# Two cached pages per item: the second page's table read and load on the GpSimd queue

## The chip, the cores and the metric

One core of a Trainium2 chip runs the whole program. The time is that of the device, in microseconds (us), of one execution. The kernel before took 1503.48, 1509.17 and 1512.21 us in three runs, median 1509.17. Engines: PE (TensorE, matrix products), DVE (VectorE), ACT (ScalarE), POOL (GpSimd), SP (SyncE, which here only issues DMAs). TensorE's clock has two levels, 1.2 and 2.4 GHz; the profile gives the granted clock as a share of the upper one.

## The reference

One step of a two-layer decoder for a prompt of 256 tokens and 8 samples with 8 new tokens each, which share all weights; 320 token columns in all. The first layer projects the input once and feeds two branches:

- an attention of 8 heads. The prompt attends to itself, with a relative bias. Each sample attends to its own 8 tokens and to 2048 cached tokens, of which the three best blocks of 256 keys per query are chosen by the product of the query with the block's mean key. The cache is paged: 128 tokens to a page, 16 pages to a sample, found by a table of page numbers;
- an mLSTM with a matrix memory, of 4 heads.

The core of the sample branch in the reference's terms:

```python
k_mean = jnp.mean(kb.astype(f32), axis=2)            # blocks of 256 keys
gate = jnp.einsum('bthd,bnhd->bhtn', q.astype(f32), k_mean)
sel_val, sel_idx = lax.top_k(gate, n_sel)            # three blocks
p = softmax(concat([s_own, s_sel]))                  # own tokens and chosen blocks
o = p_own @ v_own + p_sel @ v_sel
```

The second layer is a gated short convolution. Both end in a layer norm over a scaled residual. The outputs are the activations, the new keys and values, and the new mLSTM and convolution states.

## The kernel before

Everything that TensorE multiplies comes through one stream of items of 512 KB, each loaded into one of 11 buffers called `raw`. An item is half of a weight tile (`lin_load`, one DMA), two cached pages of keys or of values (`k_load`, `v_load`, two DMAs of 256 KB), or a state of the mLSTM (`state_item`, two DMAs of 256 KB). Weight halves are split into a high part `sh` (ACT) and a low part `sl` (DVE) before TensorE uses them (`split`); pages are used as they are.

The pages are read in four units of 4 samples and 4 heads. A unit has 32 key items (8 blocks of 256 keys for 4 samples) and 32 value items, so there are 128 items of each, and 512 page loads in all. The program puts 4 page items in a bunch and then two or three weight halves, in the order K0 K1 V0 K2 V1 K3 V2 V3 (K0: the keys of unit 0). This stage lies at about 42 to 800 us of the span; after it only weights and states are loaded.

The order on each engine is written out once, when the program is built. The loop `ahead` starts the load of an item as soon as its buffer has been freed in that order, and it calls the item's `load`. What an engine's queue holds is therefore in the order in which the functions were called, and each engine works through its queue strictly in that order. All page loads, weight loads and state loads stand in SP's queue. A page load has its page number read from the table `pt` first: `page` (L454) makes a register load on the queue's engine, register arithmetic and a check of the range (three instructions), then L461 or L469 issues the DMA.

POOL's queue holds the small transfers, in this order by the program: `rel` (L330) and `dt15` (L333), the rows of the relative bias; for each head the stores of keys `k_o` (L354, L355) and of values `v_o` (L365), and the bias rows `bt` of the prompt's head (L406, in `prompt_head`); then `hn` and `n0` (L657, L658), the mLSTM's segment mask and state, with some memsets; `kd` and `vd` (L803, L829), mLSTM moves; stores of states. In `prompt_head` the load of `bt` is the first instruction. DVE then adds it to TensorE's scores in `pS`, and TensorE transposes `pS` (out `mB` or `mC`, from `cst,pS`). The function is started after the value tile of its head has been stored.

Of the kernel before, what the change touches and what calls it, by code (L numbers as in the profile page):

```python
# [36 lines left out]
NPG = 16  # L37
NPOOL = 160
# [112 lines left out]
def trunk_kernel(ctx, tc, x_in, kc, vc, pages, cst_in, seg_in, hot_in, small_in, c0_in, n0_in, w_in,  # L151
                 y_out, k_out, v_out, cp_out, cs_out, n_out, m_out, conv_out):
    nc = tc.nc
# [35 lines left out]
    pt = pc.tile([1, NB * NPG], I32, name="pt")  # L189
# [260 lines left out]
    units = [Unit(n) for n in range(4)]  # L450
    pv_groups = [0]

    def page(b, j):
        return nc.sync.value_load(pt[0:1, b * NPG + j:b * NPG + j + 1], min_val=0, max_val=NPOOL - 1)  # L454

    def k_load(u, blk, b4):
        def f(raw):
            r = raw.rearrange("p (g f) -> p g f", g=2)
            for j in range(2):
                n = page(4 * u.quad + b4, 2 * blk + j)  # L460
                nc.sync.dma_start(r[:, j, :], kc[bass.ds(n, 1), u.half].rearrange("o p f -> (o p) f"))  # L461
        return f

    def v_load(u, b4, pp):
        def f(raw):
            r = raw.rearrange("p (g f) -> p g f", g=2)
            for j in range(2):
                n = page(4 * u.quad + b4, 2 * pp + j)
                nc.sync.dma_start(r[:, j, :], vc[bass.ds(n, 1), :, 512 * u.half:512 * u.half + 512]  # L469
                                  .rearrange("o p f -> (o p) f"))  # L470
        return f

# [1035 lines left out]
    for ft in range(KT):  # L1508
# [5 lines left out]
        o = M[:, ft, :]  # L1514
        c = 16 + ft
        g, b = small[:, S_LG + c:S_LG + c + 1], small[:, S_LB + c:S_LB + c + 1]
# [128 lines left out]
```

## Time and profile before

| | us |
|---|---|
| runs (median of 3) | 1503.48 to 1512.21 (1509.17) |
| the profiled execution | 1510.37 |
| its span | 1508.6 |
| PE busy | 1462.5 (97%) |
| DVE busy | 776.0 (51%) |
| ACT busy | 598.1 (40%) |
| POOL busy | 128.1 (8%) |

The span is the time between the first and the last instruction of the profiled execution. Busy means that an instruction was running; the times in which an engine stood still, and what ended each of them, are in the views of the waits. The DMA share is the mean busy share of the core's 16 DMA engines. An issue on SP or POOL is only the instruction that starts a DMA; its data land later.

### The profile page before, as it was taken

What the parts mean: (1) busy time and instruction counts of PE and PEld (TensorE: products, weight loads), DVE (VectorE), ACT (ScalarE), POOL (GpSimd) and SP (SyncE); (2) the same over time, 40 slices, a digit from 0 to 9 for tenths busy, and PEclk for the clock granted to TensorE, in tenths of its full rate; (3) what the DMA queues carried; (4) which work ended last, traced back from release to release, by engine and by line L of the source; (5) the groups of instructions that cost most, each with busy time, mean ns of one, the idle gap of its engine ahead of it and who ended that gap; (6) DMA issues with size and microseconds to landing.
All of it is one profiled execution on the core that took longest, in us unless ns stands there. A gap on an engine that the chain in (4) does not pass through costs nothing.

```text
span 1508.6 us, 31980 instructions
## 1 busy us (share of the span) xinstructions
PE 1462.5 (97%) x11983; PEld 1372.1 (91%) x11983; DVE 776.0 (51%) x1296; ACT 598.1 (40%) x1124; POOL 128.1 (8%) x244
## 2 busy tenths in 40 slices
PE   9899999999989999799989999999999999999998
PEld 9688889888879788699889999999999999999998
DVE  5234334433333423243256865777766666666665
ACT  5233534433233433243254444444443333333444
POOL 0200000010001010000001006223110000000000
PEclk9999999999989999999999999999999999999999
DMA  9799989989899999899884546777656444444412
GB/s 325 252 323 309 304 270 312 300 273 308 297 304 304 303 320 301 273 310 310 274 312 146 199 170 185 242 227 220 227 200 196 141 140 162 145 140 157 155 43 70
DMA packets 150957, 356.43 MB, mean 236 GB/s; under 512 B 24453, under 2 KB 30854, under 8 KB 150802
## 3 DMA queue, kind: packets, MB, share of 16 engines
q1 hardware_dynamic: 130946, 325.65, 64.3%
q0 software_dynamic: 19856, 28.74, 6.7%
q8 instruction: 94, 1.54, 0.4%
q14 instruction: 61, 0.50, 0.1%
HBM read 337.31 MB, written 16.98 MB: 235 GB/s over the span
## 4 chain that ended last, share of the span: by engine, by line
PE 74%; issue 12%; DMA 7%; ACT 2%; DVE 2%; SPq 1%; POOL 1%; ACTq 0%; POOLq 0%; DVEq 0%
PE lin L164 64%; PE kv L164 6%; DMA raw<-w_all 3%; PE mB L164 2%; DMA bt<-rel 1%; ACT sh L86 1%; PE mC L164 1%; DMA M<-x_in 1%; DVE sl L86 1%; POOL Xl L1263 1%; SPq L454 1%; PE mB L169 1%; DMA vd<-vms 1%; SPq L469 1%; DVE M L86 0%
## 5 line engine op out<-in xcount | busy, mean ns | idle before, releaser
L86 DVE TENSOR_TENSOR sl<-raw,sh 128x1024 fp32r<-128x1024 f32 (+1 forms) x341 | 412.0, 1215 | 521.0 <-ACT sh L86 518.2
L86 ACT ACTIVATE sh<-raw 128x1024 fp32r<-128x1024 f32 (+1 forms) x341 | 354.0, 1046 | 460.9 <-DMA raw<-w_all 264.0
L164 PE MATMUL lin<-Xh,sh 128*128 128x320 f32 x1648 | 526.0, 319 | 10.2 <-ACT sh L86 8.5
L164 PE MATMUL lin<-Xh,sl 128*128 128x320 f32 x1648 | 512.8, 311 | 4.7 <-DVE sl L86 4.7
L164 PE MATMUL lin<-Xl,sh 128*128 128x320 f32 x1648 | 511.8, 311 | 0.5 <-DVE Xl L86 0.5
L164 PEld LDWEIGHTS lin<-Xh,sh 128*128 128x128 f32 x1648 | 311.9, 189 | 32.5 <-issue 13.8
L164 PE MATMUL lin<-X2h,sh 128*128 128x322 f32 x1024 | 318.5, 311 | 0.0
L164 PEld LDWEIGHTS lin<-Xh,sl 128*128 128x128 f32 x1648 | 311.7, 189 | 7.0 <-DVE sl L86 6.9
L164 PE MATMUL lin<-X2l,sh 128*128 128x322 f32 x1024 | 317.8, 310 | 0.0
L164 PE MATMUL lin<-X2h,sl 128*128 128x322 f32 x1024 | 317.6, 310 | 0.0
L164 PEld LDWEIGHTS lin<-Xl,sh 128*128 128x128 f32 x1648 | 312.0, 189 | 1.6 <-DVE Xl L86 1.0
L164 PEld LDWEIGHTS lin<-X2l,sh 128*128 128x128 f32 x1024 | 193.8, 189 | 0.1
L164 PEld LDWEIGHTS lin<-X2h,sh 128*128 128x128 f32 x1024 | 192.8, 188 | 0.1
L164 PEld LDWEIGHTS lin<-X2h,sl 128*128 128x128 f32 x1024 | 192.5, 188 | 0.0
L164 PE MATMUL kv<-raw,PT 128*32 128x128 f32 x2048 | 69.0, 276 | 4.5 <-DMA raw<-vc 4.5
L164 PE MATMUL kv<-raw,qp 128*32 128x256 f32 x1024 | 65.5, 390 | 7.3 <-issue 7.3
L164 PEld LDWEIGHTS kv<-raw,PT 128*32 128x32 f32 x2048 | 54.2, 110 | 15.3 <-DMA raw<-vc 8.2
L164 PEld LDWEIGHTS kv<-raw,qp 128*32 128x32 f32 x1024 | 29.6, 111 | 30.0 <-issue 15.0
L86 ACT ACTIVATE sg<-sg 128x320 f32<-128x320 f32 x71 | 33.3, 469 | 13.1 <-DVE sg L86 11.5
L86 ACT ACTIVATE lnq<-M 128x320 f32<-128x320 f32 x30 | 14.1, 472 | 59.0 <-DVE M L86 59.0
L86 DVE SCALAR_TENSOR_TENSOR z<-lnc,ze,lin 128x320 f32<-128x320 f32 x64 | 34.7, 543 | 2.2 <-ACT ze L86 2.2
L86 DVE TENSOR_TENSOR z<-z,lny 128x320 f32<-128x320 f32 x64 | 31.5, 492 | 2.2
(311 smaller groups left out, 1006.6 us busy)
## 6 DMA issues: line engine op xcount, KB each, us to landing
raw<-w_all SPq DMA_DIRECT2D x335, 512.0 KB, 4.9
raw<-kc SPq DMA_DIRECT2D x256, 256.0 KB, 4.4
raw<-vc SPq DMA_DIRECT2D x256, 256.0 KB, 4.5
raw<-c SPq DMA_DIRECT2D x32, 256.0 KB, 5.6
xr<-c POOLq DMA_DIRECT2D x32, 256.0 KB, 4.6
cs_o<-xr POOLq DMA_DIRECT2D x32, 256.0 KB, 4.2
xr<-x_in POOLq DMA_DIRECT2D x16, 160.0 KB, 3.3
y_o<-M SPq DMA_DIRECT2D x16, 160.0 KB, 1.8
```

What stands on the lines that cost most here:

```text
L86: return fn(out, *a, **k)
L164: nc.tensor.matmul(out, lhsT=lhsT, rhs=rhs, **k)
L169: nc.tensor.transpose(out, in_, identity)
L454: return nc.sync.value_load(pt[0:1, b * NPG + j:b * NPG + j + 1], min_val=0, max_val=NPOOL - 1)
L469: nc.sync.dma_start(r[:, j, :], vc[bass.ds(n, 1), :, 512 * u.half:512 * u.half + 512] .rearrange("o p f -> (o p) f"))
L1263: nc.gpsimd.dma_start(t[32 * i:32 * i + 32, g, :], src[hd, :, row:row + 8, :])
```

## The change

In `k_load` and `v_load` the first page of an item is read from the table and loaded by SP as before, the second by POOL.

```diff
-    def page(b, j):
-        return nc.sync.value_load(pt[0:1, b * NPG + j:b * NPG + j + 1], min_val=0, max_val=NPOOL - 1)
+    def page(queue, b, j):
+        return queue.value_load(pt[0:1, b * NPG + j:b * NPG + j + 1], min_val=0, max_val=NPOOL - 1)
 
     def k_load(u, blk, b4):
         def f(raw):
             r = raw.rearrange("p (g f) -> p g f", g=2)
-            for j in range(2):
-                n = page(4 * u.quad + b4, 2 * blk + j)
-                nc.sync.dma_start(r[:, j, :], kc[bass.ds(n, 1), u.half].rearrange("o p f -> (o p) f"))
+            for j, queue in enumerate((nc.sync, nc.gpsimd)):
+                n = page(queue, 4 * u.quad + b4, 2 * blk + j)
+                queue.dma_start(r[:, j, :], kc[bass.ds(n, 1), u.half].rearrange("o p f -> (o p) f"))
         return f
 
     def v_load(u, b4, pp):
         def f(raw):
             r = raw.rearrange("p (g f) -> p g f", g=2)
-            for j in range(2):
-                n = page(4 * u.quad + b4, 2 * pp + j)
-                nc.sync.dma_start(r[:, j, :], vc[bass.ds(n, 1), :, 512 * u.half:512 * u.half + 512]
+            for j, queue in enumerate((nc.sync, nc.gpsimd)):
+                n = page(queue, 4 * u.quad + b4, 2 * pp + j)
+                queue.dma_start(r[:, j, :], vc[bass.ds(n, 1), :, 512 * u.half:512 * u.half + 512]
                                   .rearrange("o p f -> (o p) f"))
         return f
```

PE, DVE and ACT keep their order, row for row. SP loses 1024 rows and POOL gains 1024 (four for each page: the register load, a pair and a single register instruction, the DMA).

On SP before, this is one page item between the weight halves of a bunch, both pages (`raw` with its number is the buffer of one item):

```order
L226 DMA raw_1715<-w_all 128x1024
L454 TENSOR_LOAD pt_73
L454 ISA x2
L461 ISA
L461 DMA raw_1721<-kc 128x512
L454 TENSOR_LOAD pt_73
L454 ISA x2
L461 ISA
L461 DMA raw_1721<-kc 128x512
```

The last four rows are now in POOL's queue, and SP goes on with the first page of the next item.

On POOL before, these are the stores and bias rows of four prompt heads (0 to 3), of which each `bt` stands right behind its head's `v_o`:

```order
L365 DMA v_o<-vstage_1905 128x320
L406 DMA bt_2029<-rel_115 128x256
L365 DMA v_o<-vstage_2292 128x320
L406 DMA bt_2307<-rel_115 128x256
L365 DMA v_o<-vstage_2719 128x320
L406 DMA bt_2865<-rel_115 128x256
L365 DMA v_o<-vstage_3097 128x320
L406 DMA bt_3106<-rel_115 128x256
```

On POOL now, this is the end of the bunch between `v_o` and `bt` of head 2; two more pages, of the same four rows each, stand between the `v_o` row and these:

```order
L454 TENSOR_LOAD pt_73
L454 ISA x2
L461 ISA
L461 DMA raw_2795<-kc 128x512
L454 TENSOR_LOAD pt_73
L454 ISA x2
L461 ISA
L461 DMA raw_2816<-kc 128x512
L406 DMA bt_2865<-rel_115 128x256
```

At heads 0, 2, 4 and 6 four pages have moved in ahead of `bt`; at heads 1, 3, 5 and 7 `v_o` and `bt` are still adjacent, and the pages stand ahead of `v_o`.

## Rows read from the trace of the kernel before

**Rows 1.** The page's first part: busy time, share of the span, instructions.

```profile
PE 1462.5 (97%) x11983; PEld 1372.1 (91%) x11983; DVE 776.0 (51%) x1296; ACT 598.1 (40%) x1124; POOL 128.1 (8%) x244
```

**Rows 2.** Windows: us, each engine's busy us (instructions), clock, DMA share, GB/s.

```profile
60.00:800.00 740.00, 710.22 (x6915) 626.78 (x6914) 280.32 (x544) 282.75 (x596) 39.12 (x74) 0.99 0.89 299
400.00:450.00 50.00, 44.91 (x513) 36.72 (x512) 16.87 (x38) 11.80 (x22) 0.00 (x0) 0.92 0.87 298
600.00:650.00 50.00, 42.41 (x469) 36.27 (x466) 15.58 (x32) 12.07 (x20) 0.00 (x0) 0.93 0.84 273
650.00:700.00 50.00, 49.57 (x591) 45.62 (x589) 19.08 (x29) 25.13 (x58) 4.85 (x9) 1.00 0.94 324
750.00:800.00 50.00, 43.12 (x346) 38.48 (x335) 27.93 (x51) 26.76 (x49) 0.54 (x1) 0.97 0.80 293
```

**Rows 3.** What PE waited for, 400 to 800 us: total, times, longest.

```profile
PE lin L164 <- ACT sh L86: 8.5, 7, 2.1
PE lin L164 <- DVE sl L86: 4.6, 7, 0.7
PE kv L164 <- DMA raw<-vc: 4.5, 9, 1.7
```

**Rows 4.** Timeline of SP: start, us, engine, line, operation.

```profile
329.74 0.35 SPq L461 DMA_DIRECT2D raw<-kc  x1
...
623.12 8.74 SPq L469 DMA_DIRECT2D raw<-vc  x8
631.96 2.34 SPq L226 DMA_DIRECT2D raw<-w_all  x2
```

**Rows 5.** Windows of 5 us, columns as in rows 2.

```profile
630.00:635.00 5.00, 3.78 (x69) 2.56 (x67) 0.00 (x0) 0.00 (x0) 0.00 (x0) 1.00 0.64 195
690.00:695.00 5.00, 5.00 (x61) 4.76 (x60) 1.55 (x2) 2.67 (x6) 1.07 (x2) 1.00 1.00 380
```

**Rows 6.** Timeline of POOL at heads 0 and 1, idle time before in brackets.

```profile
124.99 0.54 POOL L365 DMA_DIRECT2D v_o<-vstage  x1 [42.43 <-ACT vstage L86]
125.52 0.55 POOL L406 DMA_DIRECT2D bt<-rel  x1
145.55 0.54 POOL L365 DMA_DIRECT2D v_o<-vstage  x1 [19.48 <-ACT vstage L86]
```

**Rows 7.** Timeline of DVE around the prompt heads.

```profile
136.07 0.55 DVE L86 TENSOR_SCALAR pS<-pS,st 128x128 f32<-128x128 f32 x2
...
145.17 1.22 DVE L86 TENSOR_TENSOR sl<-raw,sh 128x1024 fp32r<-128x1024 f32 x1
...
182.00 0.55 DVE L86 TENSOR_SCALAR pS<-pS,st 128x128 f32<-128x128 f32 x2
...
226.17 0.62 DVE L86 SCALAR_TENSOR_TENSOR pS<-mB,bt 128x128 f32<-128x128 f32 x2 [5.28 <-DMA bt<-rel]
```

**Rows 8.** Timeline of PE: transposes of pS at heads 0, 2, 4, 6.

```profile
139.24 0.49 PE L169 MATMUL mB<-cst,pS 128*128 128x128 f32 x3
...
186.57 0.49 PE L169 MATMUL mB<-cst,pS 128*128 128x128 f32 x3
...
231.80 0.70 PE L169 MATMUL mB<-cst,pS 128*128 128x128 f32 x3 [0.55 <-DVE pS L86]
...
294.65 0.70 PE L169 MATMUL mB<-cst,pS 128*128 128x128 f32 x3 [1.17 <-DVE pS L86]
```

**Rows 9.** Timeline of SP at the start of the page loads.

```profile
32.34 8.58 SPq L461 DMA_DIRECT2D raw<-kc  x8
```

**Rows 10.** Timeline of PE at the first key item.

```profile
51.22 1.08 PE L164 MATMUL kv<-raw,qp 128*32 128x256 f32 x8 [7.33 <-issue]
```

**Rows 11.** Window behind that stop, columns as in rows 2.

```profile
48.00:53.00 5.00, 1.78 (x20) 1.01 (x24) 3.48 (x8) 2.37 (x5) 0.66 (x1) 0.61 0.40 107
```

**Rows 12.** Timeline of POOL at the mLSTM's segment mask.

```profile
328.82 0.54 POOL L657 DMA_DIRECT2D hn<-seg  x1 [14.91 <-PE mC L164]
```

**Rows 13.** Timeline of DVE where the mask is first read.

```profile
338.84 0.81 DVE L86 TENSOR_TENSOR_SCAN M<-hn,M 4x320 f32<-4x320 f32 x1
```

## The prediction

> **What bounds the kernel now.** I read the page's busy times first: TensorE is busy for 97% of the span [rows 1], so a change pays only where TensorE stands idle or runs below full clock. The windows of 50 us say where: in 60 to 800 us, the stage of the page loads, TensorE is busy 710 of 740 us; after 800 us it is full and no page is loaded. Most of the hole lies in three windows: 400:450 with 44.91 busy, 600:650 with 42.41, 750:800 with 43.12 [rows 2]. That is 5.1 + 7.6 + 6.9 = 19.6 us of idle time, and their granted clock of 0.92, 0.93 and 0.97 takes another 50 × (0.08 + 0.07 + 0.03) = 9.0 us. The list of what TensorE waited for between 400 and 800 us names split weights (ACT `sh` 8.5, DVE `sl` 4.6) and value pages (4.5): 17.6 us of waits that go back to loads [rows 3].
>
> Are those loads late because the DMA engines are full, or because SP hands them out too slowly? In the starved stretch SP issues eight pages in 8.74 us and two weight halves in the 2.34 us behind them [rows 4], without a rest. Eight pages are 2.10 MB, so pages alone come at 2.10/8.74 = 240 GB/s. In 630:635, where TensorE starves, the DMA share is 0.64 and 195 GB/s; in 690:695, where it doesn't, 1.00 and 380 GB/s [rows 5]. So there the queue is the limit and not the engines. One page costs SP 8.74/8 = 1.09 us, though the DMA instruction itself takes 0.35 [rows 4]; the other 0.74 is the index: register load, register arithmetic, a check.
>
> At the start of the stage there is one more stop: SP gives eight pages in 8.58 us [rows 9] ahead of the weight half that TensorE needs next, and TensorE stands for 7.33 us [rows 10], with a clock of 0.61 in the five us 48:53 [rows 11].
>
> **The change part by part.** All instructions of TensorE, DVE and ACT stay in their order. Of 512 page loads 256 leave SP, each with its index step, and stand in POOL's queue at the place where they were emitted, between what POOL already carries.
>
> *SP, the gain.* Per bunch (four page items, two or three weight halves) SP loses four pages: 4 × 1.09 = 4.4 of some 11.1 us. POOL issues its four beside it, so the bytes then come as fast as the engines carry them. For the size: 600:650 moved 273 × 50 = 13.65 MB [rows 2]. At the 324 GB/s of the full window 650:700 [rows 2] that takes 42.1 us, so 7.9 of that window's 7.6 + 3.5 = 11.1 us come back, 71%. The whole recoverable sum is 17.6 + 9.0 = 26.6 us; 71% of it is 18.9. Ends: 0, if the rate doesn't rise, and 26.6. At the start the eight pages, 2.10 MB, take 5.5 us at 380 GB/s and not 8.58: 3.1 us, from ends 0 and 7.3 + 2.0 (five us at 0.61). Together 22 us, from 0 to 36. Elsewhere TensorE is not waiting for loads, and earlier ones bring nothing.
>
> *POOL, one page.* POOL loads no register in this trace. Its own issue takes 0.54 to 0.55 us [rows 6], SP's 0.35; with SP's index step that makes 0.74 + 0.55 = 1.29 us, which I take, as the same step on the nearest sequencer. From below 0.55, if the index step runs ahead of the issue; from above SP's whole cadence on top of the issue, 1.09 + 0.55 = 1.64. Less than the bare issue is excluded. Four pages are 5.2 us (2.2 to 6.6), within a bunch of 740/64 = 11.6 us: POOL keeps up.
>
> *What queues behind them: the bias rows.* Before each prompt head POOL stores `v_o` and, 0.53 us later, loads that head's bias rows `bt` [rows 6]. DVE's `pS` waits for this load, 5.28 us at head 4 [rows 7], and TensorE's transposes wait for `pS`. In the new order four pages stand between `v_o` and `bt` at heads 0, 2, 4 and 6; at the odd heads the two stay adjacent. Their delay is 5.2 us, less the slack between the end of DVE's `pS` and TensorE's use of it: at head 0 139.24 − 136.62 = 2.6, at head 2 186.57 − 182.55 = 4.0; at heads 4 and 6 TensorE waited already (0.55 and 1.17), so none [rows 7, 8]. Cost 2.6 + 1.2 + 5.2 + 5.2 = 14.2 us. A stop of such length costs clock as well: 2.0 us after the 7.33 us one [rows 10, 11]; I add it at heads 4 and 6, 4 us. Loss 18.2 us. Ends: a delay of 2.2 gives 0 + 0 + 2.2 + 2.2 = 4.4; a delay of 6.6, and 1.05 MB of pages at 380 GB/s (2.8 us) ahead of `bt` in the same DMA queue, 9.4 in all, gives 6.8 + 5.4 + 9.4 + 9.4 + 4 = 35.
>
> *The rest.* Eight pages now stand ahead of the mLSTM's segment mask `hn`: 8 × 1.29 = 10.3 us, under the 14.91 us that POOL waited there, and DVE reads it 10.0 us after its issue [rows 12, 13]: 0, and up to 5 if these pages wait for buffers. The stores `k_o` and `v_o` and the small moves `vd` and `kd` come at most a bunch's four pages later; the list of TensorE's waits names none of them: 0. POOL reads its index from the same table tile that SP reads: 0.
>
> Sum: profiled run 1510.4 − 22 + 18.2 = 1506.6. The median of the runs is 1.2 lower, so 1505.4, rounded to 1506.
>
> **Two rules weighed.** In 630:635 the engines were 0.64 busy behind a queue that never rested [rows 4, 5], and by that row a second queue helps. The Trainium skill, "DMA: Bandwidth & Descriptors", section "Issuing engines are not separate DMA queues", says that all queues run on the same 16 DMA engines and that a second issuing engine only saves the issue time, usually small beside the transfer; the trace differs here, 1.09 us of issue for 0.69 us of transfer (262 KB at 380 GB/s). By the rule the 22 us would be 0.
>
> The second bears on POOL. The `v_o` issue of 145.55 falls wholly into DVE's `sl<-raw,sh` of 145.17 to 146.39 and takes 0.54 us, as the one of 124.99 does with no such instruction beside it [rows 6, 7]. The Trainium skill, "SBUF — State Buffer", section "SBUF: two separate sides", says that the descriptors of a DMA issued by GpSimd can't be written while a DVE operation holds the port pair the two share; the row doesn't show that, though its recorded span may leave out what follows.
>
> **The rivals.**
> A, cheap pages: POOL's index step runs ahead, a page costs 0.55. Loss 4.4, gain 22 to 36: 1478 to 1492. For it: POOL was 8% busy [rows 1]. Against: every page needs its register before it issues.
> B, the transfers were the limit: no gain, loss 18.2: 1527. For it: the mean DMA share in 60:800 is 0.89 [rows 2]. Against: 0.64 just where TensorE starves.
> C, the other side, a slow POOL page: at heads 0, 2, 4 and 6 each of the four pages meets one `sl` of 1.22 us [rows 7] and waits for it. A page then costs 2.5 us, the delay is 10: 7.4 + 6.0 + 10 + 10 + 4 = 37; gain about 19 (3.15 MB per 10 us): 1527. It turns the change slower once a page costs more than some 1.8 us. [...]
> D, POOL is held: it waits 42.43 us for ACT's `vstage` ahead of a `v_o` [rows 6], and pages behind it wait too; TensorE then starves at prompt heads. If four of eight cost 4 us each more than the forecast: 1522. Against: loads go out some ten items ahead.
> That the change doesn't do what it says is excluded by the order of POOL.
>
> **How the numbers follow.** A measurement of this kernel tells about 0.5%, 7.5 us, from no change. The forecast, both effects and close to even, 0.45: 1496 to 1516, and its 0.45 splits in faster 0.20, same 0.24, slower 0.01. A 0.16, all faster. B 0.14: slower 0.11, same 0.03. C 0.15: slower 0.13, same 0.02. D 0.10: slower 0.09, same 0.01. Sums: faster 0.36, same 0.30, slower 0.34. The range from 1484 to 1530 leaves out the fast end of A and the slow ends of C and D, under 2 in 10; the forecast's own is 1496 to 1516.
>
> **What would show it.** Right: windows 400:450, 600:650 and 750:800 at 47 us or more of TensorE, a DMA share above 0.9 there, eight pages of a bunch issued in some 5 us by two queues, `bt` issued about 5 us behind `v_o` at even heads, and TensorE's waits for `pS` between 60 and 400 us grown from 3.8 us to 12 or more. The first step is wrong if the DMA share stays below 0.85 where TensorE starves, though SP rests; the second if POOL's pages follow one another by 0.6 us or by over 2 us; the forecast as a whole, if a third place appears where TensorE waits for a page that POOL issued late.

## The result: 1.2% faster, by more than forecast

The changed kernel took 1491.76 us (median of 6 runs, 1485.12 to 1497.0) against 1509.95 for the kernel before (6 runs, 1503.48 to 1514.06) measured beside it: a ratio of 0.9883, 95% interval 0.9847 to 0.9919. That is 18 us less, or 12 to 23 by the interval. The forecast was 1506, a gain of 4; the time lies in the range of 1484 to 1530, below the forecast's own 1496 to 1516. The profiled executions lie further apart than the medians, 1485.12 against 1510.37 us, so the 25 us which follow stage by stage are some 7 too many.

Windows of the changed kernel, columns as in [rows 2]:

```profile
60.00:800.00 740.00, 716.50 (x7003) 640.89 (x7002) 289.22 (x556) 289.55 (x606) 172.26 (x328) 0.99 0.85 302
100.00:350.00 250.00, 234.89 (x2191) 209.97 (x2191) 98.42 (x191) 98.93 (x217) 59.05 (x111) 0.98 0.81 283
400.00:450.00 50.00, 49.54 (x581) 43.69 (x574) 21.02 (x53) 17.05 (x40) 11.80 (x22) 1.00 0.88 305
600.00:650.00 50.00, 49.35 (x585) 44.61 (x585) 22.64 (x45) 22.14 (x47) 12.34 (x23) 1.00 1.00 375
750.00:800.00 50.00, 48.22 (x321) 47.09 (x321) 27.64 (x45) 27.46 (x50) 3.22 (x12) 1.00 0.56 200
200.00:250.00 50.00, 45.51 (x437) 40.70 (x436) 14.95 (x27) 16.02 (x31) 11.84 (x22) 0.93 0.74 260
```

The three starved windows are full: 49.54, 49.35 and 48.22 us of TensorE where [rows 2] had 44.91, 42.41 and 43.12, with the clock at 1.00. (The windows lie at fixed times, and the work has moved forward in them; the table below compares the same work.) But 100:350, the prompt heads, has only 234.89 of 250 us. The same window of the kernel before:

```profile
100.00:350.00 250.00, 243.72 (x2287) 217.22 (x2286) 100.98 (x197) 104.10 (x224) 15.92 (x31) 1.00 0.90 296
```

So TensorE lost 8.8 us of busy time there, and some clock. What TensorE waited for in the changed kernel, from 60 to 400 us and then from 400 to 800 us, in the form of [rows 3]:

```profile
PE mB L169 <- DVE pS L86: 13.9, 4, 4.7
PE kv L164 <- DMA raw<-kc: 1.8, 1, 1.8
PE mC L169 <- DVE pS L86: 1.2, 1, 1.2
```

```profile
PE lin L164 <- DVE sl L86: 2.5, 4, 0.7
...
PE lin L164 <- ACT sh L86: 1.5, 2, 0.8
```

The 17.6 us of [rows 3] have shrunk to 4.0, and no wait for value pages is left. In exchange the waits for `pS` are 13.9 + 1.2 = 15.1 us. In the kernel before they were 3.8 us from 60 to 400:

```profile
PE mC L169 <- DVE pS L86: 2.1, 3, 1.1
PE mB L169 <- DVE pS L86: 1.7, 2, 1.2
```

POOL's timeline shows why, here at head 4 (start, us, engine, line, operation, idle time before):

```profile
215.09 0.54 POOL L365 DMA_DIRECT2D v_o<-vstage  x1 [2.94 <-ACT vstage L86]
216.44 0.54 POOL L469 DMA_DIRECT2D raw<-vc  x1 [0.81 <-issue]
218.03 0.54 POOL L469 DMA_DIRECT2D raw<-vc  x1 [1.06 <-issue]
219.30 0.54 POOL L469 DMA_DIRECT2D raw<-vc  x1 [0.73 <-issue]
220.57 0.54 POOL L469 DMA_DIRECT2D raw<-vc  x1 [0.73 <-issue]
221.10 0.54 POOL L406 DMA_DIRECT2D bt<-rel  x1
```

The pages follow one another by 1.27 us (once 1.59), and `bt` is issued 221.10 − 215.09 = 6.0 us behind `v_o`; in [rows 6] it was 0.53. DVE and TensorE pay for it. The timeline of DVE, then that of TensorE, to be set against the last row of [rows 7] (5.28 us of waiting) and the third of [rows 8] (0.55):

```profile
227.43 0.62 DVE L86 SCALAR_TENSOR_TENSOR pS<-mB,bt 128x128 f32<-128x128 f32 x2 [10.36 <-DMA bt<-rel]
```

```profile
231.93 0.95 PE L169 MATMUL mB<-cst,pS 128*128 128x128 f32 x3 [4.49 <-DVE pS L86]
```

TensorE executes the same 11983 matmuls in the same order in all traces (four at one place apart), so the time of one and the same matmul can be subtracted, stage by stage (my subtraction of the recorded starts, us gained over the kernel before in each stretch of its time axis; negative is lost):

| kernel | 0 to 55 | 55 to 125 | 125 to 350 | 350 to 425 | 425 to 500 | 500 to 652 | 652 to 1400 | sum |
|---|---|---|---|---|---|---|---|---|
| changed | 8.6 | −1.7 | −11.3 | 0.1 | 8.1 | 14.3 | 7.0 | 25.1 |
| changed, bias rows ahead | 8.3 | −1.6 | 9.0 | 0.1 | 6.4 | 14.0 | 8.5 | 44.5 |
| before, fixed pages | 7.8 | 0.3 | 9.0 | 0.1 | 8.7 | 13.5 | 9.1 | 48.6 |
| before, no range check | 4.6 | −0.2 | 7.5 | 0.1 | 2.9 | 9.7 | 7.5 | 32.1 |
| before, bias rows on ACT | 1.9 | 0.3 | −9.8 | 0.0 | −2.1 | −0.7 | 1.1 | −9.2 |
| before, bias rows ahead | 2.6 | −0.1 | 5.3 | −1.8 | −0.4 | −0.5 | −0.1 | 5.0 |
| changed, key pages on SP | 0.5 | −0.2 | −7.6 | 0.1 | 4.6 | 9.5 | 5.2 | 12.2 |

The first row is the result in one line: about 36 us come back at the start and behind 425 us, 11 are lost at the prompt heads. The other rows are the experiments below. How far one profiled run may differ from another without a cause shows in the row "before, bias rows ahead": its edit touches nothing ahead of 80 us, and still 2.6 us stand there.

### The profile page after: what moved, and what is told of

It is laid out like the page before. It is cut to its first block, busy times and chain, and to the rows that moved or that the text cites. A ratio compares the mean times of both kernels' runs of the same rounds, so it can differ in the third digit from the quotient of the medians.

```text
span 1483.5 us, 32279 instructions
## 1 busy us (share of the span) xinstructions
PE 1450.4 (98%) x11983; PEld 1368.5 (92%) x11983; DVE 776.7 (52%) x1296; ACT 598.2 (40%) x1124; POOL 265.5 (18%) x500
## 4 chain that ended last, share of the span: by engine, by line
PE 77%; DMA 9%; issue 7%; DVE 2%; POOLq 1%; ACT 1%; POOL 1%; SPq 1%; ACTq 0%; DVEq 0%
PE lin L164 66%; PE kv L164 6%; DMA raw<-w_all 5%; PE mB L164 2%; DMA bt<-rel 2%; PE mC L164 1%; POOLq L454 1%; ACT sh L86 1%; PE mB L169 1%; DVE sl L86 1%; DMA raw<-kc 1%; DMA raw<-vc 1%; DMA pt<-pages 1%; POOL raw L461 0%; PE mA L169 0%
## 5 line engine op out<-in xcount | busy, mean ns | idle before, releaser
L164 PEld LDWEIGHTS lin<-Xh,sh 128*128 128x128 f32 x1648 | 310.2, 188 | 24.0 <-issue 14.2
L469 POOL DMA_DIRECT2D raw<-vc x128 | 68.9, 538 | 223.8 <-PE kv L164 104.0
L461 POOL DMA_DIRECT2D raw<-kc x128 | 69.4, 542 | 208.5 <-issue 69.8
L164 PEld LDWEIGHTS kv<-raw,qp 128*32 128x32 f32 x1024 | 29.1, 109 | 25.1 <-issue 7.9
L1290 POOL DMA_DIRECT2D cs_o<-xr x32 | 17.7, 552 | 159.5 <-DVE xr L86 153.7
```

The source lines that it names most:

```text
L164: nc.tensor.matmul(out, lhsT=lhsT, rhs=rhs, **k)
L461: queue.dma_start(r[:, j, :], kc[bass.ds(n, 1), u.half].rearrange("o p f -> (o p) f"))
L469: queue.dma_start(r[:, j, :], vc[bass.ds(n, 1), :, 512 * u.half:512 * u.half + 512] .rearrange("o p f -> (o p) f"))
L1290: nc.gpsimd.dma_start(cs_out[hd, b], c)
```

## Experiments

**Is it the place of the bias rows?** Two kernels test it. One issues `bt` on ACT:

```diff
-        nc.gpsimd.dma_start(bt, bass.AP(tensor=rel.tensor, offset=rel.offset + 512 * h, ap=[[1, 128], [1, 256]]))
+        nc.scalar.dma_start(bt, bass.AP(tensor=rel.tensor, offset=rel.offset + 512 * h, ap=[[1, 128], [1, 256]]))
```

> The changed kernel, with one line altered: the bias rows bt are issued by ACT instead of GpSimd. Theory 1 (the changed kernel loses time at prompt heads 0, 2, 4 and 6 because bt stands behind four page loads in GpSimd's in-order queue): TensorE's waits for pS between 60 and 360 us fall from 15.1 us to 4 or less, bt is issued under 1 us after the value tile is ready, and the time falls by the 8 to 13 us that the trace loses between 125 and 310 us: 1479 to 1485. Rival (bt is late because the software DMA queue and the hardware queues now share the engines, wherever it is issued): it lands 6 to 8 us after its issue and in all as late as before; 1490 to 1494.

1470.34 us against 1507.02, ratio 0.9759 (0.9743 to 0.9775). That is 36.7 us below the kernel before, where the changed kernel was 18.2 below the one measured beside it: 18 us from this one line, more than the 8 to 13 expected. The waits for `pS`:

```profile
PE mB L169 <- DVE pS L86: 4.8, 2, 3.1
```

The other leaves `bt` on GpSimd, but issues it where the value tile is made, ahead of its store:

```diff
     def post_v(h):
...
+            bts[h] = p1_.tile([128, 256], F32, name="bt", tag="bt", bufs=2)
+            nc.gpsimd.dma_start(bts[h], bass.AP(tensor=rel.tensor, offset=rel.offset + 512 * h, ap=[[1, 128], [1, 256]]))
             v = p1_.tile([128, N], F32, name="vstage", tag="vstage", bufs=2)
...
     def prompt_head(h, x_bank):
-        bt = p1_.tile([128, 256], F32, name="bt", tag="bt", bufs=2)
-        nc.gpsimd.dma_start(bt, bass.AP(tensor=rel.tensor, offset=rel.offset + 512 * h, ap=[[1, 128], [1, 256]]))
+        bt = bts.pop(h)
```

> The changed kernel with the bias rows bt still on GpSimd, but issued right ahead of the value store of their head, so that no page stands between. This changes the place in the queue alone. Theory 1 (place in the queue): the waits for pS fall from 15.1 us to under 5, as with bt on ACT, and the time comes to 1466 to 1475. If it was the software DMA queue (pages and bias rows share its rings) and not the place, the rows still land late: the waits stay over 10 us and the time at 1483 to 1492.

1468.61 against 1507.13, ratio 0.9752 (0.9731 to 0.9772). Its POOL timeline at head 4:

```profile
204.88 0.54 POOL L471 DMA_DIRECT2D raw<-vc  x1 [0.72 <-issue]
205.41 0.54 POOL L365 DMA_DIRECT2D bt<-rel  x1
208.37 0.54 POOL L368 DMA_DIRECT2D v_o<-vstage  x1 [2.42 <-ACT vstage L86]
```

`bt` now goes out 2.96 us before `v_o`, behind four pages as before, but while `v_o` would still have waited for ACT. No wait for `pS` is left on TensorE; what remains from 60 to 400 us is one line:

```profile
PE kv L164 <- DMA raw<-kc: 1.5, 2, 1.1
```

Same queue, same kind of DMA, only another place in the order: the loss is the place. By the table it is 9.0 + 11.3 = 20.3 us at the prompt heads, and by the medians too (38.5 us below the kernel before in place of 18.2).

**Controls on the kernel before.** Both moves of `bt`, made without any page on GpSimd.

> The kernel before with bt issued ahead of the value store on GpSimd: the control of the run above. What the same move is worth where no page stands between: the 3.8 us of waits for pS at most, and some clock: 1502 to 1510. And it tells whether the 10 us that bt on ACT cost the kernel before came from ACT's hardware queue (one page load on SP waited 4.2 us for the bias rows there): if so, nothing of that is seen here; if the earlier rows themselves upset the order, 1512 or more.

1505.88 against 1507.13, ratio 0.9996 (0.9979 to 1.0014): nothing, as expected, and 3 us at most by the interval. So of the 20 us that the same edit brings the changed kernel nearly all are the repair of the change's own damage.

> The kernel before, with bt issued by ACT. In the kernel before no page stands between the value store and bt, so theory 1 expects next to nothing: 1506 to 1512. If ACT's queue lands the rows earlier by itself (a hardware queue against the software queue), up to 3.8 us, the waits for pS of the kernel before, could go: 1506. If it is slower than 1514, ACT's own time for the issue matters and the gain of the same edit on the changed kernel is understated.

1517.62 against 1507.02, ratio 1.0065 (1.0049 to 1.0081): 10 us slower. Such a time I had put down beforehand to ACT's own time for the issue. What SP waited for from 60 to 400 us (total, times, longest):

```profile
SPq L461 <- DMA bt<-rel: 12.8, 3, 5.3
...
SPq L469 <- DMA bt<-rel: 5.2, 1, 5.2
...
SPq L226 <- DMA bt<-rel: 1.4, 1, 1.4
```

SP's loads wait 12.8 + 5.2 + 1.4 = 19.4 us for bias rows to land, though they don't need them. In the program DMAs of SP and ACT take turns in the same eight completion semaphores, and a load whose turn comes waits until the last DMA of that semaphore has landed: head 0's rows, issued at 124.17, landed at 129.48, and the page load with the same semaphore went out at 129.50. TensorE's waits show how that reaches it:

```profile
PE mB L164 <- ACT pP L86: 5.4, 1, 5.4
PE mC L164 <- ACT pP L86: 4.4, 1, 4.4
```

ACT had stood for the late weight half ahead of this `pP`, 9.75 us at head 0:

```profile
143.76 1.06 ACT L86 ACTIVATE sh<-raw 128x1024 fp32r<-128x1024 f32 x1 [9.75 <-DMA raw<-w_all]
```

Those two waits are 9.8 us, and the table's loss at the prompt heads is 9.8; in the kernel before `pP` cost 2.0. ACT's own time for an issue is 0.33 us, too little for this. That it is not the bias rows' earlier issue follows from the control above. No run with separate semaphores was made.

**Is it SP's time per page?** The kernel before with page numbers fixed in the program: `page` returns a constant, and the loads are plain slices. This leaves out the read of the table, and the pages are then taken in the order in which they lie.

```diff
-        return nc.sync.value_load(pt[0:1, b * NPG + j:b * NPG + j + 1], min_val=0, max_val=NPOOL - 1)
+        return b * NPG + j
...
-                nc.sync.dma_start(r[:, j, :], kc[bass.ds(n, 1), u.half].rearrange("o p f -> (o p) f"))
+                nc.sync.dma_start(r[:, j, :], kc[n:n + 1, u.half].rearrange("o p f -> (o p) f"))
```

> The kernel before with the page numbers fixed in the program, all 512 loads still on SP; the read of the page table is left out. Theory 1 (SP hands pages out too slowly, 1.09 us each, of which 0.74 us is the index step): eight pages are issued in about 3 us, the starved stretches at 400:450, 600:650, 750:800 and the stop at the start go, and with nothing added on GpSimd the whole gain of about 36 us comes: 1470 to 1480. Rival (two queues feed the engines better than one, whatever the issue costs): the stretches stay starved: 1500 to 1510.

1459.3 against 1507.02, ratio 0.9686 (0.9672 to 0.9701): 48 us, more than the 27 to 37 expected, with one queue. SP's timeline in the stretch of [rows 4], and the window of [rows 2]:

```profile
588.41 5.55 SPq L469 DMA_DIRECT2D raw<-vc  x8
```

```profile
600.00:650.00 50.00, 49.13 (x560) 44.75 (x550) 21.46 (x40) 26.63 (x58) 2.73 (x5) 1.00 0.97 349
```

The same eight pages are issued in 5.55 us, not 8.74 (about 3 were expected; SP now also waits for buffers and landings); TensorE has 49.13 us and the engines carry 349 GB/s at a share of 0.97. A second DMA queue is not what was missing.

**A smaller dose.** The kernel before without the check of the page number's range:

```diff
-        return nc.sync.value_load(pt[0:1, b * NPG + j:b * NPG + j + 1], min_val=0, max_val=NPOOL - 1)
+        return nc.sync.value_load(pt[0:1, b * NPG + j:b * NPG + j + 1])
```

> The kernel before, all pages on SP, without the check of the page number's range (two of the index step's instructions, FUSED_REGOPS of 0.15 us and SEQ_ASSERT of 0.02, go). A smaller dose of what fixed page numbers took away. Theory 1 (SP's time per page is the limit): the cadence falls from 1.09 to 0.85 to 0.95 us, eight pages take 1.1 to 1.9 us less, and between a third and nearly all of the gain of fixed numbers (48 us) comes: 1462 to 1492. Rival (the two queues, not SP's time): 1504 to 1510.

1471.75 against 1507.13, ratio 0.977 (0.9745 to 0.9795). SP's timeline and the window:

```profile
600.84 6.72 SPq L469 DMA_DIRECT2D raw<-vc  x8
```

```profile
600.00:650.00 50.00, 48.02 (x517) 44.15 (x516) 21.59 (x43) 22.95 (x50) 0.57 (x1) 0.97 0.98 350
```

6.72/8 = 0.84 us for a page instead of 1.09. A quarter of a microsecond off each of 512 pages brings 35 us, three quarters of all that fixed numbers brought: SP was only a little too slow, and a little faster is nearly as good as much faster. These pages still come from the table in its order, so the order of the fixed pages is not what most of the 48 us hang on.

**Key pages or value pages.** The changed kernel with key pages all on SP:

```diff
-            for j, queue in enumerate((nc.sync, nc.gpsimd)):
+            for j, queue in enumerate((nc.sync, nc.sync)):
                 n = page(queue, 4 * u.quad + b4, 2 * blk + j)
```

> The changed kernel with the second page on GpSimd for value items alone; all key pages on SP. From the shift between the two traces, stretch by stretch: without the 6.9 us of the start, without the loss at heads 0 and 2 (about 5), with the loss at heads 4 and 6 (about 8) and with most of the 29 us of 425 to 450, 500 to 650 and 750 to 775: 1486 to 1494. If key pages matter as much as value pages in the late stretches: above 1497.

1496.22 against 1507.02, ratio 0.9927 (0.9907 to 0.9947): 2 us over the stated interval. What TensorE waited for from 60 to 400 us:

```profile
PE mB L169 <- DVE pS L86: 9.9, 2, 5.5
PE mC L169 <- DVE pS L86: 1.3, 2, 0.8
```

Heads 0 and 2 are free (their `bt` is issued 0.53 us behind `v_o`), heads 4 and 6 are not, and the gain of the start is gone, as the positions in the queues say. Behind 425 us the table gives 4.6 + 9.5 + 5.2 = 19.3 us in place of the changed kernel's 29.4. I had expected most of the 29; key pages count there too, if less than value pages.

**Cheaper pages on both queues.** The changed kernel with fixed page numbers on SP and on GpSimd, by the edit of the kernel with fixed pages above.

> The changed kernel with the page numbers fixed in the program, on both queues; the read of the page table is left out. GpSimd then has its bare issue of 0.54 us for a page and bt comes 4 x 0.54 + 0.54 = 2.7 us behind the value store and not 6. Theory 1: the waits for pS fall from 15.1 us to 5 or 8, the loads have no limit left in SP: 1466 to 1476, between 3 and 12 us above the 1459 of fixed page numbers on SP alone, since bt is still late. If pages through GpSimd cost something else beside bt (landing, rings), over 1478.

1481.18 against 1507.13, ratio 0.9828 (0.981 to 0.9846): 5 us over what was expected. `bt` is issued only 2.7 us behind `v_o` at head 4 (212.09 and 214.83), yet TensorE waits for `pS` about as the theory said:

```profile
PE mB L169 <- DVE pS L86: 7.9, 4, 3.9
PE mC L169 <- DVE pS L86: 0.8, 1, 0.8
```

What I missed seems to be the landing. The line of the `bt` tile's loads, first of this kernel and then of the changed kernel:

```profile
DMA to landing us min/median/max: 4.0/7.9/9.9
```

```profile
DMA to landing us min/median/max: 4.3/6.3/8.8
```

Median 7.9 us and up to 9.9, against 6.3 and up to 8.8: what the shorter queue of GpSimd saves is partly lost in the landing. At the even heads, behind four pages, the rows took 8.4, 8.7, 8.9 and 9.9 us here and 7.5, 6.5, 6.2 and 8.8 in the changed kernel; at the odd heads the two are alike (4.0 to 7.5 and 4.3 to 7.4). That fits pages whose data stand ahead of the rows' in the same DMA queue, my upper end for this term, but no run takes it apart: rows issued by ACT, with no page in their queue, took up to 9.9 us as well. This kernel also loses some 3 us at 25 and 3 to 4 near 450 and 640 us against fixed pages on SP alone; why was not looked into.

**The best of both.** The changed kernel with bias rows ahead and no range check on either queue, and the kernel before with the same two edits and one queue.

> Three edits at once: pages on both queues, bias rows ahead of the value store, and no check of the page number's range on either queue. If SP's issue time and the bias rows are all that is left, the time comes near the 1459 of fixed page numbers: 1457 to 1466. If a second queue brings nothing once SP's page is cheaper, it stays where one queue without the check is, 1466 to 1473.

> The kernel before (all pages on SP) with bias rows ahead of the value store and without the range check: the rival of the run above with one queue alone. The earlier bias rows were worth nothing in the kernel before, and the waits for pS are only 0.2 us without the check, so 1468 to 1474, as without the check alone; it would be under 1464 only if bias rows still bind.

1468.75, ratio 0.975 (0.9724 to 0.9777), and 1469.58, ratio 0.9752 (0.9724 to 0.9779). The first missed its 1457 to 1466, and came where "a second queue brings nothing once SP's page is cheaper" had put it; the second came as expected. Two queues with the check and `bt` out of the way (1468.61), two without it, and one without it end within 1 us, 2.5% below the kernel before. The remaining 9 us to fixed page numbers are the read of the table itself, what it delays, or the order of the pages; no run separates them.

## Why the prediction came out where it did

**What bounds the kernel: right.** That SP's 1.09 us a page was the limit in the starved stretches, and not the DMA engines, is shown by the runs with fixed pages and without the check. Rival B falls with it: with two queues the engines carried 375 GB/s over 600:650, where [rows 2] have 324 at most. The DMA share above 0.9 that I asked for came in one of the three windows only, 0.88, 1.00 and 0.56; the third is no test, since the last page number is read at 730 us now (below). A window of 5 us within it, columns as in [rows 5]:

```profile
615.00:620.00 5.00, 5.00 (x65) 4.41 (x55) 0.26 (x1) 0.00 (x0) 1.61 (x3) 1.00 1.04 396
```

**The gain: the step that was mis-sized.** I put it at 22 us out of 0 to 36. With `bt` out of the way it is 38.5 us by the medians (1507.13 − 1468.61), beyond the upper end. Three things were too small. I scaled by the 324 GB/s of 650:700, a window that was full because TensorE asked for no more; 600:650 now moves 375 GB/s at a share of 1.00. So not 71% of the stretches came back but all of it: 8.1 + 14.3 + 7.0 = 29.4 us behind 425 against 18.9 forecast, from an upper end of 26.6. The start gave 8.6 − 1.7 = 6.9 and not 3.1, for which I had let all eight pages' bytes pass ahead of the weight half. That two queues spare it half of them is not the reason, for fixed pages on one queue gave 7.8 + 0.3 there; the reason is open, and 2.6 us of such a figure can be chance. And I looked for starved time behind 400 us and at the start only; between 125 and 350 us the run with fixed pages gains 9.0 us, with `bt` where it was. TensorE's waits in the kernel before, from 60 to 400 us, are 6.2 us in all, for `pS`, `pP` and `vstage`; with fixed pages the list is empty. Bias rows ahead alone bring the kernel before 3 us at most, so part of the 9.0 comes with the loads; how much is open.

**A page on GpSimd: right.** 1.29 us was forecast, 1.27 measured (219.30 to 220.57), with the index step's register load about as long as SP's. The price of SP's page was read a little low: the 8.74 us of [rows 4] begin at the first issue and so hold eight issues but seven index steps. From issue to issue SP took 1.10 us at least and 1.15 in the median, by which POOL's page would have been 1.30 to 1.35. Rows of both queues in the changed kernel, from 60 to 800 us (durations in ns, least, median, most):

```profile
L454 POOLq TENSOR_LOAD <-pt x243: 283/288/716, 60.8 to 725.8; - x122
L454 SPq TENSOR_LOAD <-pt x239: 263/271/689, 63.8 to 730.3; - x120
```

Rival A's price of 0.55 and rival C's of 2.5 are both refuted by this cadence; that the time fell into the span that A gave, 1478 to 1492, is luck. DVE's two-input `sl` beside these issues didn't lengthen them: 69 of POOL's 256 page issues overlap one, and take 0.54 us (median) like the other 187. The Trainium skill's page "SBUF — State Buffer", section "Who interferes with whom", doesn't ask for a price here: it gives its rule for DVE operations in a two-port mode, and infers that `tensor_tensor`, which `sl` is, leaves the writing of descriptors alone. So the trace agrees with the page, and I had weighed its rule on an operation that it doesn't cover. The other rule weighed, in the Trainium skill's page "DMA: Bandwidth & Descriptors", section "Issuing engines are not separate DMA queues", holds in its first half: two queues didn't beat one once the issue was cheap. Its "usually small" doesn't hold for these pages: taking 0.25 us off the issue of each brought 35 us.

**The delay of the bias rows: right in place and in size.** 5.2 us of pages between `v_o` and `bt` were forecast at heads 0, 2, 4 and 6; the changed kernel has 6.0, 7.6, 6.0 and 6.1 from one issue to the other, against 0.5 to 0.8 before. The loss was put at 18.2 us; it is 20.3 by the table and by the medians. TensorE's waits at these four heads are 3.3, 1.5, 4.5 and 4.7 us, 12.2 more than before, where 14.2 were forecast. Its waits for `pS` rose to 15.1 us in all where I asked for 12 or more, and the clock fell to 0.93 in 200:250, 50 × 0.07 = 3.5 us of the 4 set aside for it.

**The rest: right but for one place.** No wait for `hn`, `vd`, `kd` or a store appears among TensorE's. But the third place that I named as a sign against the forecast, a wait of TensorE for a page that POOL issued late, did appear: the 1.8 us for `raw<-kc` shown above. POOL was not held by `vstage`, as in rival D, but by the relative bias at the head of its queue, for which the prediction has no term. POOL, then TensorE:

```profile
44.29 0.54 POOL L330 DMA_DIRECT2D rel<-S  x1 [14.58 <-DVE om L86]
46.73 4.62 POOL L333 DMA_DIRECT2D dt<-rel  x8 [1.90 <-DMA rel<-S]
...
58.51 0.54 POOL L461 DMA_DIRECT2D raw<-kc  x1 [0.79 <-DMA raw<-kc]
```

```profile
65.98 0.64 PE L164 MATMUL kv<-raw,qp 128*32 128x256 f32 x8 [1.81 <-DMA raw<-kc]
```

SP had issued the first page of this item at 46.41; POOL issued the second at 58.51, and it landed at 65.93.

So a gain that was too small by 16 us and a loss too small by 2 made a forecast that was too high by 14. Its sign hung on a difference of two terms of some 20 us each; I had the ends of both (0 to 36, 4 to 35) and took the gain near its middle, although the argument that SP was the limit said that its upper end was the likelier one.

## What to carry to other kernels

Here a queue without rest stood ahead of engines that starved a little, and a small relief brought nearly the whole starved time back. Scale such a gain by the highest rate that any short window reached, not by a window in which nobody asked for more. What moves to another in-order queue lands between that queue's old work: list what stands behind each insertion, and put the loads that someone waits for ahead of the store that blocks. And before spreading an issue over two queues look at what the issue consists of; here leaving out the range check brought 35 us, and the second queue 18, or 38 with `bt` out of its way.

## What the runs showed of the hardware

The check of a page number's range, two small instructions on SP's sequencer (0.15 and 0.02 us in the trace), was worth 35 us of 1507: a page took 0.25 us less without it. A DMA on ACT's queue held back loads on SP's, 19.4 us of waits in one kernel, through completion semaphores that the program shares between the two. And bias rows on GpSimd's queue landed later, 7.9 us (median), with pages of 0.54 us each ahead of them than with pages of 1.27, 6.3; whether the pace of that queue or the load of the engines does it is not shown.
